# Layer A of a three-layer network: the projections' input kept by position classes modulo 4

## Chip, core and metric

One core of one Trainium2 chip runs the whole kernel. The metric is device time in microseconds (us), the median of several runs; lower is better.

## What is computed

A sequence of 512 positions with 1024 features goes through two layers, each a mixer and a mixture of experts with modulation from a condition vector, and then a third block with a state space and a pooling branch. All of it is float32. The change concerns the mixer of the first layer, "layer A":

```python
A_DILATED = ((128, 1), (512, 4), (2048, 16))   # window, dilation of the three groups

def dilated_group_attention(q, k, v, bias_table, window, dilation):
    """Query t attends to t - m*dilation, m = 0..window/dilation. Keys are gathered by stride:
    the sequence is split into `dilation` residue classes ..."""

def dilated_mixer(h, w_in, w_out, q_gain, k_gain, rel_bias):
    proj = (h @ w_in).reshape(b, s, A_N_GROUPS, 3, A_HEADS_PER_GROUP, HEAD_DIM)
    for g, (window, dil) in enumerate(A_DILATED):
        q = rmsnorm(proj[:, :, g, 0], q_gain) * ATTN_SCALE
        k = rmsnorm(proj[:, :, g, 1], k_gain)
        v = proj[:, :, g, 2]
        o, l = dilated_group_attention(q, k, v, tab, window, dil)
    ...
    wts = jax.nn.softmax(jnp.stack(lses, axis=0), axis=0)
    o = jnp.sum(wts[..., None] * outs, axis=0)
    return o.reshape(b, s, A_GROUP_WIDTH) @ w_out
```

Each group has 16 heads of 64 features. Group 0 attends to neighbouring positions; groups 1 and 2 attend within classes of positions that are equal modulo 4 (and 16).

## The kernel before

The normalized and modulated input of layer A lies transposed in SBUF, features on partitions, as `hT`: two float32r tiles `hThi` and `hTlo` of 128 x 8 x 512 whose sum is the float32 value. They are made in mix_a: tiles of x are normalized, transposed by TensorE and copied to `xT` (L2095), scaled and shifted to `hfull` (L2127), and split in two. Their 512 positions stand in natural order.

`dilated` goes through 24 units, for each of 8 pairs of heads the groups 0, 1, 2. A unit (`qkv_proj`) projects q, k and v of a pair of heads, 384 columns, for four tiles of 128 positions. Each tile adds up 8 blocks of 128 features, each in three terms (high x high, high x low, low x high): 96 pairs of a weight load and a matmul in a unit, all recorded at L153 (`split3`). The stationary operand of each is a slice of `hT`, the moving one the weights. Which positions make a tile is set in `qkv_part`: in group 0 tile t is the positions 128 t to 128 t + 127, in groups 1 and 2 it is every fourth position from t on:

```python
ts = slice(t, None, 4) if strided else slice(t * P, (t + 1) * P)
```

From a tile's sums in PSUM (`mm`, two buffers), ScalarE copies q and k to `raw` (L410), squares them to `sq` (L412) and copies v to `vhi` (L413); VectorE makes `vlo` (L414) and reduces the squares to `qss` (L415). Between the tiles the next unit's weights `wst` are split into `whi` and `wlo` (L315, L316). At the unit's end q and k are multiplied with the inverse norms (L425).

Attention runs as steps between the projections' matmuls. `qk_rows` transposes q and k (L435); for group 0 they are split into `qTh`, `qTl`, `kTh`, `kTl` (L448 to L452). `attn_near` computes group 0's scores (L536), the softmax pieces (L461, L462) and, in `attn_values`, the transposes of the probabilities (L474) and the products with v (L153, `av`) into `UN` (L551). `attn_far` does the same for groups 1 and 2 and writes its result in natural order to `UR`, at a step of four floats (L607). `merge` joins both. Besides, 20 blocks of the modulation of later stages are summed up on VectorE from `w_ada` (`ast`, `adacc`, L240 to L248).

TensorE's order is set by hand: `weave` mixes the projection's steps and the attention's steps by costs written in the source (490 for three pairs). The orders of the other engines and of SP's queue, which issues nearly all transfers, are set by the scheduler of the tile framework; each engine works in order. Layer B uses the same `qkv_proj` with natural tiles.

Of the kernel before, what the change touches and what calls it, by code (L numbers as in the profile page):

```python
# [9 lines left out]
F32 = mybir.dt.float32  # L10
# [10 lines left out]
S = 512  # L21
# [79 lines left out]
class Held:  # L101
    """Takes an engine's calls and keeps them for later."""
# [9 lines left out]
class Kernel:  # L112
# [47 lines left out]
    def rsqrt_exp(self, pool, out, v, n, tag, after):  # L160
        """exp(-ln(v) / 2), then a Newton step."""
        nc = self.nc
        t = self.t(pool, [P, n], F32, tag + "_t", 2)
        self.need_ln(after)
        with self.tc.issue_after(self.ln_table.ins):
            nc.scalar.activation(out, v, AF.Ln)
        nc.scalar.activation(out, out, AF.Exp, scale=-0.5)
        nc.vector.tensor_mul(t, out, out)
        nc.vector.scalar_tensor_tensor(t, t, -0.5, v, op0=ALU.mult, op1=ALU.mult)
        nc.vector.scalar_tensor_tensor(out, t, 1.5, out, op0=ALU.add, op1=ALU.mult)  # L170

# [11 lines left out]
    def first_columns(self, pool):  # L183
        """What the first modulation needs."""
# [47 lines left out]
    def ada_steps(self, pool, l, cb, st_tag="ast", n_st=2, later=False, n_acc=2, n_pe=0):  # L232
        """The last n_pe rows of blocks are TensorE's, the others are summed up on VectorE first."""
# [40 lines left out]
    def row(self, pool, col, tag, bufs=1):  # L274
        """A vector held one value per partition, as a row on every partition."""
# [11 lines left out]
    def tile_norm(self, pool, x):  # L287
        """1 / rms of every row of a tile."""
# [34 lines left out]
    def w_unit(self, w, base, ncols, qkv):  # L323
        """[k, 3 x 128 columns] of a projection: a pair of heads' q, k and v. The splits are left to do, piece by piece."""
# [11 lines left out]
    def w_rows(self, w, k0, nk, base, ncols, n, width=None, todo=None):  # L336
        """[k0 .. k0+nk, n columns] of a matrix, in one piece."""
# [9 lines left out]
    def weave(self, bg, fg):  # L347
        """bg yields costs (or what it has to wait for); fg holds (lane, steps, delay), and steps yield cost and delay.
        A lane's steps run one after the other."""
# [39 lines left out]
    def qkv_part(self, p, w, hT, strided, t, k):  # L389
        ts = slice(t, None, 4) if strided else slice(t * P, (t + 1) * P)  # L390
# [4 lines left out]
    def qkv_proj(self, pool, w, hT, strided, u, g, nv, todo, begun=None, n_raw=2):  # L395
        """begun: sums over the first features, where they have been started."""
# [3 lines left out]
        vlo = self.t(pool, [P, NT, P], F32R, f"vlo{g}", nv)  # L400
        raw = self.t(pool, [P, NT, 2, P], F32, "raw", n_raw)
        ss = self.t(pool, [P, 4 * NT], F32, "qss", n_raw)
        u.update(v=(vhi, vlo), raw=raw, ss=ss)
        for t in range(NT):
            p = ps[t] if ps else self.mm()
            for k in range(k0, KC):
                self.qkv_part(p, w, hT, strided, t, k)
# [3 lines left out]
            sq = self.t(pool, [P, 256], F32, "sq", 2)  # L411
# [4 lines left out]
            if t < NT - 1:  # L416
                for x in todo[t:t + 1] if t < 2 else todo[t:]:
                    self.split_weights(*x)
                yield 490
        v = self.t(pool, [P, 4 * NT], F32, "qv", 2)  # L420
# [7 lines left out]
    def qk_rows(self, pool, u, l, g, split):  # L428
        """q and k with heads' features on partitions."""
        nc = self.nc  # L430
        out = []
        for j, nm in enumerate(("qT", "kT")):
# [11 lines left out]
            else:  # L444
                hi = self.t(pool, [P, S], F32R, f"{nm}h{g}", 1)
                lo = self.t(pool, [P, S], F32R, f"{nm}l{g}", 1)
                if j == 0:
                    nc.scalar.activation(hi, p, AF.Copy, scale=gain)  # L448
                    nc.vector.scalar_tensor_tensor(lo, p, gain, hi.bitcast(F32), op0=ALU.mult, op1=ALU.subtract)
                else:  # L450
                    nc.scalar.activation(hi, p, AF.Copy)
                    nc.vector.tensor_sub(lo, p, hi.bitcast(F32))  # L452
# [5 lines left out]
    def softmax_piece(self, p, bias, out, z, d, n):  # L458
        """out = exp(p + bias - max), z = -max, d = the sum."""
# [4 lines left out]
    def transpose_split(self, pool, blocks, n, tag, q=P):  # L464
        """Transposes of q x 128 blocks of a float32 tile, in two parts."""
# [32 lines left out]
    def bias_rep(self, head):  # L498
        """The row of a head once per partition, so that rows shifted by one each can be read."""
# [15 lines left out]
    def attn_near(self, pool, u, hp, st):  # L515
        """Group 0 over its pair of heads: each block of 128 queries against its own and the block before."""
# [4 lines left out]
        yield from self.qk_rows(pool, u, 0, 0, True)  # L521
# [32 lines left out]
    def attn_values(self, pool, f, blocks, hs, terms, out):  # L554
        """Transposes of the probabilities' blocks, then their products with v; out(h, [64, S])."""
# [21 lines left out]
    def attn_far(self, pool, u1, u2, hp, st, out):  # L577
        """Groups 1 and 2 over their pairs of heads, by classes of positions mod 4; then the merge."""
# [34 lines left out]
    def merge(self, pool, UN, UR, st, out):  # L613
        """One softmax over both kinds of keys from their maxima and sums."""
# [62 lines left out]
    def dilated(self, keep, pool, hT, oT, first, begun, extra):  # L677
# [5 lines left out]
        def bg():  # L683
            nxt = first
            for i, (hp, g) in enumerate(units):
# [13 lines left out]
                if i >= back:  # L699
                    yield lambda p=hist[i - back][1], g=g: p.get("near" if g == 0 else "far")  # L700
                yield from self.qkv_proj(pool, cur[0], hT, g != 0, us[g], g, 2 if g == 1 else 1, nxt[1] if i + 1 < len(units) else [],
                                         None if i else begun)
# [33 lines left out]
    def out_start(self, keep, oT, w, done, scored):  # L736
        """All but the last heads' part of the first columns; done(k): those heads are through, scored(): all scores are."""
# [35 lines left out]
    def out_final(self, pool, x, mT, w, g):  # L773
        """x plus the last projection, its RMS norm, and out."""
# [56 lines left out]
    def route_in(self, h, hT, ks, rw, out):  # L831
        """Some columns' part in a tile's logits."""
# [9 lines left out]
    def route_tiles(self, pool):  # L842
        """What the routes are collected in."""
# [7 lines left out]
    def route_tile(self, pool, lg, R, t):  # L851
        """A tile's experts: its group, and the two best in it."""
# [5 lines left out]
        def first_max(v, m, o):  # L858
            """Largest of four, and a one-hot of the first place where it stands."""
# [20 lines left out]
    def route_rank(self, R, t):  # L880
        """Each token's rank with its experts, from one (zero: not its own)."""
# [6 lines left out]
    def route_counts(self, pool, R):  # L888
        """The experts' counts, and whether one is above the places."""
# [11 lines left out]
    def route_gates(self, pool, lg, R):  # L901
        """The gates, in three parts."""
# [26 lines left out]
    def token_list(self, pool, rk, idx, q=P):  # L929
        """By place, of q, the token whose rank it is (out of range where there is none)."""  # L930
# [27 lines left out]
    CAP = 96    # places of an expert; tokens beyond them go through overflow()  # L958

    def expert_loads(self, l):  # L960
        """Loads, six pieces an expert: two each of its gate, up and down."""
# [57 lines left out]
    def expert_hidden_T(self, pool, hid, w):  # L1019
        """Transposed: in two parts where the weights are, or as it is."""  # L1020
# [19 lines left out]
    def expert_out(self, pool, hT, d, idx, gate, R):  # L1040
        """Products with the down weights, times the gate and the modulation, added to x in DRAM."""
# [12 lines left out]
    def overflow(self, pm, R, hd, l):  # L1054
        """Tokens beyond an expert's places, 128 at a time, for any counts: run only where there are some."""
# [83 lines left out]
    def moe_route(self, x, l, rows, steps):  # L1139
        """steps makes x, a tile at a time."""  # L1140
# [54 lines left out]
    def moe(self, R, after):  # L1195
        """after() is called among the experts, for what the next layer can have early."""
# [77 lines left out]
    def normed_T(self, pool, xd, rows, hT):  # L1274
        """Tile by tile: the RMS norm (times a row, plus a row), transposed, in two parts."""
# [22 lines left out]
    def forget_rows(self, pool, hT):  # L1298
        """Minus the running sums of log sigmoid(f), per head: [16, S] in DRAM."""
# [906 lines left out]
```

## Time and profile before

| | |
|---|---|
| median of 3 runs | 1909.9 us (1907.71 to 1918.23) |
| span of the profiled execution | 1907.5 us, 2.4 us less than the median of the runs |
| TensorE busy | 92% of the span |
| VectorE, ScalarE, GpSimd busy | 67%, 48%, 6% |
| layer A's attention | from about 50 to 740 us |

The profiled execution has a time of its own only as that span, from its first to its last instruction. Engines are named PE (TensorE matmuls), PEld (TensorE's weight loads, which overlap the matmuls), DVE (VectorE), ACT (ScalarE), POOL (GpSimd) and SP (the queue that issues transfers). A matmul's recorded duration overlaps its neighbours'; what a pair of load and matmul costs is read from the step between two starts. A row of the waits names who waited for whom, the sum, how often and the longest. The granted clock is TensorE's, as a share of 2.4 GHz.

### The profile page before, as it was taken

How to read it: one execution, taken by the hardware profiler on the slowest of the kernel's cores; microseconds unless marked ns; L12 is line 12 of the kernel's file. 1: busy time of each engine (PE TensorE's matmuls, PEld its weight loads, DVE VectorE, ACT ScalarE, POOL GpSimd, SP SyncE). 2: the span in 40 equal slices, each digit the busy share in tenths (PEclk: the TensorE clock that was granted, in tenths of full speed). 3: DMA queues.
4: the chain of work that ended last, by engine and by line, in shares of the span. 5: the costliest groups of instructions: out<-in, count | busy, mean ns of one | idle time of the engine just before them, and what ended most of it. 6: DMA issues, size and time to landing. Idle time of an engine off the chain costs nothing. (4 is left out here: it accounts for less than half of the span.)

```text
span 1907.5 us, 30333 instructions
## 1 busy us (share of the span) xinstructions
PE 1753.2 (92%) x11022; PEld 1567.3 (82%) x11023; DVE 1280.8 (67%) x3181; ACT 920.1 (48%) x1978; POOL 119.5 (6%) x95
## 2 busy tenths in 40 slices
PE   5989999999999999699978999999599968999998
PEld 3989999999999998577757888979487748788886
DVE  6747657665765555788755758765687755998674
ACT  4535444453544454365634555554365544444443
POOL 1000000000000000122310000000123210000000
PEclk9999999999999999799989999989699988999999
DMA  8785535444453213699964321216499964333332
GB/s 282 224 263 151 158 108 155 144 142 128 142 160 106 84 56 117 205 300 311 304 182 115 110 55 56 78 34 211 134 321 316 304 179 120 94 103 95 100 112 87
DMA packets 283390, 302.45 MB, mean 159 GB/s; under 512 B 30751, under 2 KB 232075, under 8 KB 283228
## 3 DMA queue, kind: packets, MB, share of 16 engines
q1 hardware_dynamic: 275676, 283.49, 47.7%
q0 software_dynamic: 7552, 16.89, 4.0%
q8 instruction: 91, 1.49, 0.3%
q14 instruction: 71, 0.58, 0.1%
HBM read 283.42 MB, written 34.71 MB: 167 GB/s over the span
## 5 line engine op out<-in xcount | busy, mean ns | idle before, releaser
L153 PE MATMUL mm<-whi,hThi 128*128 128x384 f32 (+2 forms) x1128 | 438.7, 389 | 12.3 <-DVE vlo L414 9.1
L153 PE MATMUL mm<-whi,hTlo 128*128 128x384 f32 (+2 forms) x1128 | 413.7, 367 | 0.7
L153 PE MATMUL mm<-wlo,hThi 128*128 128x384 f32 (+2 forms) x1128 | 412.7, 366 | 0.0
L153 PEld LDWEIGHTS mm<-whi,hThi 128*128 128x128 f32 x1128 | 284.5, 252 | 20.8 <-DVE vlo L414 9.4
L153 PEld LDWEIGHTS mm<-whi,hTlo 128*128 128x128 f32 x1128 | 286.5, 254 | 5.9 <-DVE hTlo L728 3.0
L153 PEld LDWEIGHTS mm<-wlo,hThi 128*128 128x128 f32 x1128 | 287.6, 255 | 1.9 <-issue 0.6
L316 DVE TENSOR_TENSOR wlo<-wst,whi 128x768 fp32r<-128x768 f32 (+2 forms) x200 | 200.5, 1011 | 73.0 <-ACT whi L315 71.3
L315 ACT ACTIVATE whi<-wst 128x768 fp32r<-128x768 f32 (+2 forms) x200 | 176.3, 891 | 98.4 <-PE mm L153 64.4
L316 DVE TENSOR_TENSOR ehl<-est,ehl 128x1024 fp32r<-128x1024 f32 x144 | 175.7, 1222 | 51.4 <-ACT ehl L315 50.8
L315 ACT ACTIVATE ehl<-est 128x1024 fp32r<-128x1024 f32 x144 | 152.0, 1057 | 98.4 <-PE sc L153 31.6
L153 PE MATMUL mm<-ehl,xTh 128*96 128x256 f32 x960 | 178.4, 287 | 0.0
L248 DVE SCALAR_TENSOR_TENSOR adacc<-ast,csil,adacc 128x512 f32<-128x512 f32 x168 | 126.0, 750 | 54.6 <-DMA ast<-in_w_ada_dram 52.8
L153 PE MATMUL mm<-ehl,xTl 128*96 128x256 f32 x480 | 135.9, 283 | 0.0
L153 PEld LDWEIGHTS mm<-ehl,xTh 128*96 128x96 f32 x960 | 134.7, 165 | 0.0
L415 DVE TENSOR_REDUCE qss<-sq 128x4 f32<-128x256 f32 x128 | 53.0, 414 | 102.0 <-ACT sq L412 101.7
L410 ACT ACTIVATE raw<-mm 128x256 f32<-128x256 f32 x126 | 48.1, 382 | 145.3 <-PE mm L153 145.0
L153 PE MATMUL mm<-hThi,whi 128*128 128x512 f32 (+1 forms) x288 | 108.1, 375 | 0.7 <-ACT sza L1875 0.6
L153 PE MATMUL mm<-hTlo,whi 128*128 128x512 f32 (+1 forms) x288 | 106.7, 371 | 0.5 <-DVE hTlo L310 0.3
L153 PE MATMUL mm<-hThi,wlo 128*128 128x512 f32 (+1 forms) x288 | 106.5, 370 | 0.0
L153 PEld LDWEIGHTS mm<-ehl,xTl 128*96 128x96 f32 x480 | 79.0, 165 | 0.0
L1214 POOL MEMSET xg<- 96x1024 f32 x6 | 5.5, 951 | 1127.3 <-PE sc L153 1127.3
L954 POOL DMA_INDIRECT xd<-y,tidx x32 | 66.9, 2091 | 123.0 <-DVE hTl L1036 95.3
(486 smaller groups left out, 3543.5 us busy)
## 6 DMA issues: line engine op xcount, KB each, us to landing
ast<-in_w_ada_dram SPq DMA_DIRECT2D x192, 256.0 KB, 3.0
wst<-in_a_w_in_dram SPq DMA_DIRECT2D x192, 192.0 KB, 3.6
est<-in_w_gate_dram SPq DMA_DIRECT2D x64, 512.0 KB, 10.6
est<-in_w_up_dram SPq DMA_DIRECT2D x60, 512.0 KB, 11.3
wst<-in_w_in_dram SPq DMA_DIRECT2D x32, 512.0 KB, 4.0
est<-in_w_down_dram SPq DMA_DIRECT2D x30, 512.0 KB, 9.8
esp<-in_w_down_dram SPq DMA_DIRECT2D x30, 512.0 KB, 11.2
wst<-in_b_w_in_dram SPq DMA_DIRECT2D x64, 192.0 KB, 3.7
```

The costliest lines, as they stand in the source:

```text
L153: self.nc.tensor.matmul(out, lhsT=l, rhs=r, start=n_first and i == 0, stop=n_last and i == nt - 1)
L248: last = nc.vector.scalar_tensor_tensor(acc, st, self.csil[:, k:k + 1], acc, op0=ALU.mult, op1=ALU.add)
L315: nc.scalar.activation(hi, st, AF.Copy)
L316: nc.vector.tensor_sub(lo, st, hi.bitcast(F32))
L410: nc.scalar.activation(raw[:, t].rearrange("p a b -> p (a b)"), p[:, :256], AF.Copy)
L415: nc.vector.tensor_reduce(ss[:, 4 * t:4 * t + 4], sq.rearrange("p (g d) -> p g d", d=HD), axis=AX.X, op=ALU.add)
L954: self.nc.gpsimd.indirect_dma_start(out=dst, out_offset=bass.IndirectOffsetOnAxis(ap=idx, axis=0), in_=src, in_offset=None, bounds_check=S ...
L1214: nc.gpsimd.memset(xg, 0.0)
```

## The change

The transposed input of layer A is kept by classes of positions modulo 4: first all positions with remainder 0, then 1, 2 and 3. Every tile of every group is then 128 neighbouring columns of `hT`. Group 0's results are put back in natural order: q and k as they are split after their transposes, written at a step of four floats, v through a tile in DRAM, written in natural order by one transfer and read back by another, for each of its two halves. These four transfers of a pair of heads are issued on SP. One scratch tile, `sq`, goes from two buffers to one, and group 0's values get two more tiles, `vch` and `vcl`. All other lines of the diff take out comments and docstrings.

```diff
-    def qkv_part(self, p, w, hT, strided, t, k):
-        ts = slice(t, None, 4) if strided else slice(t * P, (t + 1) * P)
+    def qkv_part(self, p, w, hT, t, k):
+        ts = slice(t * P, (t + 1) * P)
...
-    def qkv_proj(self, pool, w, hT, strided, u, g, nv, todo, begun=None, n_raw=2):
+    def qkv_proj(self, pool, w, hT, u, g, nv, todo, begun=None, n_raw=2, regroup=False):
...
+        vout = vhi, vlo
+        if regroup:
+            vhi = self.t(pool, [P, NT, P], F32R, f"vch{g}", 1)
+            vlo = self.t(pool, [P, NT, P], F32R, f"vcl{g}", 1)
...
-        u.update(v=(vhi, vlo), raw=raw, ss=ss)
+        u.update(v=vout, raw=raw, ss=ss)
...
-            sq = self.t(pool, [P, 256], F32, "sq", 2)
+            sq = self.t(pool, [P, 256], F32, "sq", 1)
...
+        if regroup:
+            for nm, src, dst in zip("hl", (vhi, vlo), vout):
+                vd = self.t(self.dp, [S, P], F32, "vd" + nm, 2)
+                nc.sync.dma_start(vd.rearrange("(n r) d -> n r d", r=4), src.bitcast(F32))
+                nc.sync.dma_start(dst.bitcast(F32), vd.rearrange("(b p) d -> p b d", p=P))
...
-    def qk_rows(self, pool, u, l, g, split):
+    def qk_rows(self, pool, u, l, g, split, regroup=False):
+        ro = (lambda x: x.rearrange("p (n r) -> p r n", r=4)) if regroup else (lambda x: x)
+        ri = (lambda x: x.rearrange("p (r n) -> p r n", r=4)) if regroup else (lambda x: x)
...
-                    nc.scalar.activation(hi, p, AF.Copy, scale=gain)
-                    nc.vector.scalar_tensor_tensor(lo, p, gain, hi.bitcast(F32), op0=ALU.mult, op1=ALU.subtract)
+                    nc.scalar.activation(ro(hi), ri(p), AF.Copy, scale=gain)
+                    nc.vector.scalar_tensor_tensor(ro(lo), ri(p), gain, ro(hi.bitcast(F32)), op0=ALU.mult, op1=ALU.subtract)
                 else:
-                    nc.scalar.activation(hi, p, AF.Copy)
-                    nc.vector.tensor_sub(lo, p, hi.bitcast(F32))
+                    nc.scalar.activation(ro(hi), ri(p), AF.Copy)
+                    nc.vector.tensor_sub(ro(lo), ri(p), ro(hi.bitcast(F32)))
...
-        yield from self.qk_rows(pool, u, 0, 0, True)
+        yield from self.qk_rows(pool, u, 0, 0, True, True)
...
-                yield from self.qkv_proj(pool, cur[0], hT, g != 0, us[g], g, 2 if g == 1 else 1, nxt[1] if i + 1 < len(units) else [],
-                                         None if i else begun)
+                yield from self.qkv_proj(pool, cur[0], hT, us[g], g, 2 if g == 1 else 1, nxt[1] if i + 1 < len(units) else [],
+                                         None if i else begun, regroup=g == 0)
...
-            proj = lambda hp, wu, todo: self.qkv_proj(pq, wu[0], hT, False, hist[hp], 0, DL["nvb"], todo, n_raw=DL["nrb"])
+            proj = lambda hp, wu, todo: self.qkv_proj(pq, wu[0], hT, hist[hp], 0, DL["nvb"], todo, n_raw=DL["nrb"])
...
-                        nc.scalar.activation(xT[:, 4 * i:4 * i + 4, t * P:(t + 1) * P], p.rearrange("p (a b) -> p a b", b=P), AF.Copy)
+                        xc = xT[:, 4 * i:4 * i + 4].rearrange("p k (r n) -> p k r n", r=4)
+                        nc.scalar.activation(xc[:, :, :, t * 32:(t + 1) * 32], p.rearrange("p (k n r) -> p k r n", k=4, r=4), AF.Copy)
```

## Rows read from the trace of the kernel before

**Rows 1.** the page's busy time of TensorE: share of the span, instructions

```profile
PE 1753.2 (92%) x11022; PEld 1567.3 (82%) x11023; DVE 1280.8 (67%) x3181; ACT 920.1 (48%) x1978; POOL 119.5 (6%) x95
```

**Rows 2.** windows: each engine's busy us (x instructions), granted clock, DMA share, GB/s

```profile
60.00:120.00 60.00, 57.82 (x312) 56.73 (x312) 34.02 (x79) 26.92 (x70) 0.00 (x0) 1.00 0.86 258
120.00:131.00 11.00, 5.50 (x20) 5.50 (x21) 6.55 (x14) 1.15 (x5) 0.00 (x0) 0.69 0.83 256
131.00:700.00 569.00, 567.48 (x3681) 554.83 (x3680) 357.50 (x921) 278.53 (x729) 0.00 (x0) 1.00 0.44 132
1062.00:1300.00 238.00, 231.74 (x1600) 201.43 (x1598) 160.58 (x551) 129.55 (x326) 0.00 (x0) 0.96 0.21 63
```

**Rows 3.** weight loads in order of time, group 1: start, duration, engine, line

```profile
60.27 0.33 PEld L153 LDWEIGHTS mm<-whi,hTlo 128*128 128x128 f32 x1
...
70.79 0.33 PEld L153 LDWEIGHTS mm<-whi,hTlo 128*128 128x128 f32 x1
```

**Rows 4.** the same view, group 0's second unit

```profile
113.49 0.19 PEld L153 LDWEIGHTS mm<-wlo,hThi 128*128 128x128 f32 x1
...
117.31 0.19 PEld L153 LDWEIGHTS mm<-whi,hTlo 128*128 128x128 f32 x1
```

**Rows 5.** windows, columns as in rows 2: one period of three units

```profile
459.90:542.90 83.00, 83.00 (x538) 81.25 (x537) 54.24 (x138) 40.56 (x107) 0.00 (x0) 1.00 0.47 140
```

**Rows 6.** weight loads at the stop in group 0's second unit

```profile
125.50 0.29 PEld L153 LDWEIGHTS mm<-whi,hThi 128*128 128x128 f32 x1 [8.00 <-DVE vlo L414]
125.66 0.34 PEld L153 LDWEIGHTS mm<-wlo,hThi 128*128 128x128 f32 x1
...
129.51 0.33 PEld L153 LDWEIGHTS mm<-wlo,hThi 128*128 128x128 f32 x1
```

**Rows 7.** VectorE in order of time at that stop

```profile
123.62 0.75 DVE L248 SCALAR_TENSOR_TENSOR adacc<-ast,csil,adacc 128x512 f32<-128x512 f32 x1 [3.90 <-DMA ast<-in_w_ada_dram]
```

**Rows 8.** windows, columns as in rows 2: DMA share early and later

```profile
60.00:70.00 10.00, 10.00 (x43) 10.00 (x44) 7.52 (x20) 4.43 (x13) 0.00 (x0) 1.00 0.97 284
160.00:170.00 10.00, 10.00 (x75) 9.35 (x75) 6.58 (x18) 4.65 (x14) 0.00 (x0) 1.00 0.34 107
```

**Rows 9.** tiles: duration min/median/max ns, first and last start, forms

```profile
L607 ACT ACTIVATE UR<-av x16: 1067/1088/1112, 159.7 to 733.4; 64x512 f32<-64x512 f32 x16
L551 ACT ACTIVATE UN<-av x16: 588/591/594, 100.4 to 692.0; 64x512 f32<-64x512 f32 x16
L452 DVE TENSOR_TENSOR kTl<-tp,kTh x8: 691/692/692, 74.4 to 657.6; 128x512 fp32r<-128x512 f32 x8
```

**Rows 10.** in order of time: fourth pair of heads, keys, first scores

```profile
325.74 0.69 DVE L452 TENSOR_TENSOR kTl<-tp,kTh 128x512 fp32r<-128x512 f32 x1 [1.07 <-ACT kTh L451]
...
331.84 0.19 PEld L536 LDWEIGHTS sc<-kTh,qTh 64*128 64x128 f32 x2 [0.18 <-issue]
```

**Rows 11.** DMA issues: how many, KB each, median us from issue to landing

```profile
ud<-u SPq DMA_DIRECT2D x4, 256.0 KB, 4.1
yP<-yqd SPq DMA_DIRECT2D x4, 256.0 KB, 3.7
```

**Rows 12.** fourth pair of heads, group 0: last values made, their first product

```profile
315.56 0.29 DVE L414 TENSOR_TENSOR vlo<-mm,vhi 128x128 fp32r<-128x128 f32 x1
...
348.81 0.15 PEld L153 LDWEIGHTS av<-pTh,vhi 128*64 128x64 f32 x1
```

**Rows 13.** SP's waits, 150 to 700 us: us in total, times, longest

```profile
SPq L240 <- DVE adacc L246: 105.9, 15, 11.3
```

**Rows 14.** tile xT: its copies, and what reads them first

```profile
L2095 ACT ACTIVATE xT<-tp x8: 580/597/597, 19.2 to 28.8; 128x512 f32<-128x512 f32 x8
L2127 ACT ACTIVATE hfull<-xT,mod,scol x4: 798/799/813, 33.2 to 35.3; 128x512 f32<-128x512 f32 x4
```

**Rows 15.** waits, 50 to 100 us: us in total, times, longest

```profile
ACT sq L412 <- DVE qss L415: 1.7, 1, 1.7
```

More of the change, by code (lines that the diff above doesn't have):

```diff
@@ L406, in qkv_proj @@
             for k in range(k0, KC):
-                self.qkv_part(p, w, hT, strided, t, k)
+                self.qkv_part(p, w, hT, t, k)
                 if k < KC - 1:
```

## The prediction

> **What bounds the kernel now.** I read the page's busy times first: TensorE is busy for 1753.2 us of a 1907.5 us span [rows 1]. A mean over stages with different limits says little, so the table of windows comes next. Over layer A's attention the reader should look at one pair of numbers: between 131 and 700 us TensorE is busy for 567.48 of 569 us at the full granted clock (1.00, which is 2.4 GHz), with VectorE at 357.50 us (63%), ScalarE at 278.53 us (49%) and the DMA engines at 0.44 [rows 2]. TensorE runs back to back there, so what its instructions cost is what this stage costs. Only the start differs: from 60 to 131 us the DMA engines are at 0.86 and 0.83, and TensorE stands still once.
>
> The third view is TensorE's weight loads in order of time. In qkv_part the input's 128 positions are the stationary operand, loaded anew for each matmul of 384 columns. In a unit of group 1 (positions `t, t+4, ...`) a load takes 0.33 us and the next starts 0.2338 us later: from 60.27 to 70.79 us there are 45 steps, 10.52 / 45 [rows 3]. In a unit of group 0 (128 neighbouring positions) of the same tiles hThi and hTlo, with the same matmul, a load takes 0.19 us and the step is 0.1736 us: from 113.49 to 117.31 us, 22 steps, 3.82 / 22 [rows 4]. The only thing in the code that differs between these stretches is the step between positions. So groups 1 and 2 are bound by the load of the stationary operand, and group 0 is not.
>
> The Trainium skill, page "TensorE: Matmul & The Clock Gate", section "LDWEIGHTS (loading the stationary operand)", gives a load's time from its number of columns alone, and would have both loads alike; the rows differ by 0.14 us in duration, so the measurement decides against it here. Its page "SBUF — State Buffer", section "Door 1: The DMA port swizzle", says that SBUF is read in lines of 16 bytes and that a read which moves to a new line each time pays; four floats are such a line, and the rows agree with that.
>
> **The change, part by part.**
>
> *Contiguous loads.* Two groups of 8 pairs of heads are 16 units, each of 4 tiles x 8 feature blocks x 3 terms = 96 pairs of load and matmul: 1536 pairs. Each should fall from 0.2338 to 0.1736 us: 1536 x 0.0602 = 92.5 us, all on the path that sets the end, since TensorE has no gaps for it to fall into. Group 0's units keep their 0.1736 us. TensorE's order is written by hand from costs in the source, none of which changes, so the same instructions follow in the same order.
>
> *What is late next.* A period of three units (459.9 to 542.9 us) has 83.00 us of TensorE, 54.24 us of VectorE and 40.56 us of ScalarE [rows 5]. TensorE loses 2 x 96 x 0.0602 = 11.6 us of it, which leaves 71.4 us; VectorE would go to 76%. It stays under TensorE, but the slack of every hand-over shrinks. Two rows bound what TensorE then idles: this stage's own 1.5 us in 569 (0.3%, about 1.5 us of the shorter stage), and layer B, where the same projection runs with contiguous loads among attention and TensorE is busy 231.74 of 238 us [rows 2], so 2.6% idle, or about 13 us of the stage that is left (569 less 81). I take 4 us, nearer to this stage's own row, because the instructions are its own.
>
> *The crowded start.* At 117.5 us TensorE stops for 8.00 us on vlo [rows 6], because VectorE, which works in order, has stood 3.90 us for a modulation weight on its way in [rows 7]; after it 12 steps take 0.321 us each at the lower clock (the window's mean granted clock is 0.69 [rows 2]), which adds about 2 us. DMA share is 0.97 in the ten microseconds from 60 and 0.34 from 160 [rows 8]. The two strided units before that stop save 11.6 us, but data that arrive no sooner make the stop longer by as much as TensorE came early. From the one side nothing is lost and the stop of 10 us even goes, from the other all 11.6 us are given back. I take half, 5.8 us.
>
> *Queries and keys of group 0 put back in order.* Per pair of heads two ScalarE and two VectorE operations write 512 elements at a step of four floats. ScalarE's nearest rows are UR, written with that very step, at 1.09 us, and UN, the same size written densely, at 0.59 us [rows 9]; so +0.50 us each, 8 us over 16 on an engine that is half idle. No VectorE operation of before writes so; kTl takes 0.69 us dense [rows 9], and I bound the extra by zero and one more 0.69 us, at most 11 us in 16, and take ScalarE's +0.50. On the path they count only as latency: kTl starts at 325.74 us and the scores that need it at 331.84 us [rows 10], so some 5.4 us of cover, of which about 27 pairs x 0.06 = 1.6 us go with faster projections and some 2 us with the four slower steps. What is left, 1.8 us, hides it; with VectorE behind by more than that, it costs at most 1 to 2 us a pair of heads. I put it at zero, with the 4 us above as its reserve.
>
> *Values of group 0 through DRAM.* Per pair of heads SP gets four more transfers of 256 KB, a write and a read back for each half. The nearest rows are such a round trip in the last block: 4.1 us to land written, 3.7 us read back [rows 11]. Both halves in line are 15.6 us. The values are ready 0.29 us after 315.56 and their first product starts at 348.81 us [rows 12]: 33 us of cover, less some 6 us for the 100 faster pairs between. So TensorE never waits for them. What can wait is what stands behind them on SP: a read that waits for its write holds up the modulation's and projections' weights for some 4 us, twice a period. SP already stands for up to 11.3 us at a time for a free buffer [rows 13] without TensorE stopping after 131 us. The four transfers are 1 MB among the 11.6 MB that 140 GB/s moves in 83 us. Cost: between zero and 2 x 4 us a period if VectorE has no slack, so up to 64 us; I take zero, as the row with the longer SP wait does no harm.
>
> *Small ones.* The eight xT copies (0.60 us each, the last at 28.8 us) now read and write in steps; +0.5 us each delays the last to about 33 us, just where hfull starts at 33.2 us [rows 14], so 0 to 1 us. With one sq buffer, ScalarE's square waits for VectorE's reduction of the tile before, 4.2 us earlier at least (24 pairs x 0.1736); with two it waited once, for 1.7 us [rows 15]. Layer B shares this line: 0 to 2 us there. Both at zero.
>
> **Sum.** -92.5 + 5.8 + 4.0 = -82.7 us. The profiled span of 1907.5 lies 2.4 us under the median of the runs, 1909.9, and I count the same distance again: 1909.9 - 82.7 = 1827 us.
>
> **The rivals.**
> *Better than the sum*: the stop at 117 us goes altogether and nothing idles: 1909.9 - 92.5 - 10 = 1807. For it: group 0's stretches already run without gaps. Against it: the DMA shares of the start. Chance 0.07.
> *A new wait takes the gain*: the chain of the stop (a late weight holds VectorE, vlo holds TensorE, then the lower clock), now fed by SP's round trips, recurs each period at 8 + 2 us. Four of eight give 1827 + 40 = 1867, all eight 1907. For it: VectorE's queue is in order and does wait for these weights. Against it: the DMA engines stand at 0.44 after 131 us. Chance 0.10.
> *It doesn't do what it says*: the load's time hangs on something other than the step (by the columns rule above, it would). The stage stays, and the additions cost 0 to 8 us: 1910 to 1918. Against it: same tiles, same matmul, 0.2338 against 0.1736. Chance 0.03.
> *Slower*: the values come back late. The cover is 27 us, the round trips 15.6; if SP holds the read back behind a blocked load, every microsecond over 27 is TensorE's, and it decides at 27 + 11.6 = 39 us, where the period is as long as before. At 45 us, 8 x 6 = 48 us longer: 1958. It needs about 29 us of queueing; the waits above reach 11.3. Chance 0.03.
> The forecast itself has 0.77.
>
> **How the numbers follow.** The forecast's own range is 1818 (nothing given back) to 1848 (11.6 and 13 us given back, 8 us of the small ones). The range reaches to the better case at 1807 and into the new wait at 1860. A measurement of this kernel tells about 0.5% (9.5 us) from no change. Faster by more: 0.77 + 0.07 + 0.08 of the new wait = 0.92. Within: 0.02 of it and 0.02 of the third = 0.04. Slower: 0.04.
>
> **What would show it.** In the profile after, the loads of all qkv units step by 0.174 us and none lasts 0.33 at the full clock; layer A's attention is about 80 us shorter; TensorE's busy share there stays above 97%; the strided writes take about 1.1 us; the values land long before their product. The prediction is wrong if TensorE's waits for vlo, scores or values add up to more than some 20 us in that stage, or if the DMA share of the start reaches 1 and the first period keeps its length.

## The result, and the profile after

The changed kernel takes 1849.28 us (median of 4 runs, 1845.19 to 1858.89) against 1911.37 us of the kernel before (4 runs, 1907.71 to 1918.23): a ratio of 0.9667, 95% interval 0.964 to 0.9694. The time lies inside the range, 22 us above the 1827 us that were forecast, and 1 us above what the forecast itself allowed (1818 to 1848). The profiled execution spans 1846.8 us, 60.7 us less than before.

First the page of the kernel after, busy time by engine: beside [rows 1] TensorE's busy time fell by 87.5 us, while VectorE's and ScalarE's grew by 1.8 and 6.4 us.

```profile
span 1846.8 us, 30370 instructions
PE 1665.7 (90%) x11022; PEld 1469.2 (80%) x11023; DVE 1282.6 (69%) x3181; ACT 926.5 (50%) x1978; POOL 121.0 (7%) x95
```

Then its weight loads in order of time, in a unit of group 1, where [rows 3] had 0.33 us (start, duration, engine, line):

```profile
59.90 0.19 PEld L153 LDWEIGHTS mm<-whi,hThi 128*128 128x128 f32 x1
...
66.48 0.19 PEld L153 LDWEIGHTS mm<-whi,hTlo 128*128 128x128 f32 x1
```

From the first to the last are 38 steps in 6.58 us, 0.173 us each: the step of [rows 4]. Over the whole steady stretch the loads of `mm` have a mean of 188 ns. The mechanism does what the prediction said.

The windows of the kernel after (stretch, length, then busy us and instructions of PE, PEld, DVE, ACT, POOL, granted clock, DMA share, GB/s) show what came of it; [rows 2] has the same view of before:

```profile
60.00:130.00 70.00, 57.39 (x355) 54.99 (x354) 41.81 (x93) 29.96 (x78) 0.00 (x0) 0.90 0.91 280
130.00:160.00 30.00, 27.29 (x204) 25.48 (x204) 22.70 (x57) 16.25 (x41) 0.00 (x0) 1.00 0.81 247
160.00:650.00 490.00, 473.58 (x3540) 451.07 (x3540) 347.43 (x889) 276.14 (x705) 0.00 (x0) 1.00 0.52 154
475.90:549.70 73.80, 71.62 (x538) 68.43 (x537) 54.34 (x139) 41.40 (x106) 0.00 (x0) 1.00 0.57 170
549.70:620.10 70.40, 70.36 (x538) 68.30 (x537) 44.76 (x123) 41.28 (x106) 0.00 (x0) 1.00 0.36 112
```

TensorE no longer runs back to back: it is idle for 16.4 of 490 us in the steady part. The last two lines are two neighbouring periods of three units. In the first VectorE still sums up modulation blocks; in the second there are none left, VectorE is busy 9.6 us less, and TensorE idles 0.04 us instead of 2.2.

The best ruler is the tile `oT`: its product of `UN` and `UR` closes each pair of heads, eight times (duration, first and last start). Of the kernel after, the sixth and the seventh:

```profile
L672 DVE TENSOR_TENSOR oT<-UN,UR x1: 683/683/683, 549.7 to 549.7; 128x512 f32<-128x512 f32 x1
L672 DVE TENSOR_TENSOR oT<-UN,UR x1: 685/685/685, 620.1 to 620.1; 128x512 f32<-128x512 f32 x1
```

All eight, read in the same way, in us (the third line is the last experiment below):

| | first pair ends | five periods, to the sixth | sixth to seventh | to the eighth |
|---|---|---|---|---|
| before | 184.1 | 415.7 | 81.7 | 57.4 (at 738.9) |
| after | 178.0 | 371.7 | 70.4 | 50.1 (at 670.2) |
| after, without most of the modulation sums | 160.0 | 352.5 | 70.5 | 50.1 (at 633.1) |

Layer A's attention ends 68.7 us earlier. The period without modulation gained 11.3 us, nearly the 11.6 us that 192 pairs were to give; each of the five periods with modulation gained only 8.8; and the start gained 6.1.

This ruler is good to about a microsecond. It stands on VectorE, and in the kernel before, the seventh product comes a little earlier in TensorE's order: its sixth-to-seventh stretch holds 526 TensorE instructions, against 538 in the kernel after.

```profile
599.80:681.50 81.70, 81.70 (x526) 80.02 (x524) 44.52 (x122) 40.53 (x106) 0.00 (x0) 1.00 0.27 80
```

Read at the same load of TensorE's order in both kernels, the start gains 7.3 us, the five periods 44.5, the sixth period 12.1 and the rest 4.7.

Later stages do the same work in both kernels. From `oT` to the first read of layer B's mixer there are 259.9 us before and 260.5 after, in the mixer of layer B 299.0 and 307.3, in the rest 609.7 and 608.8. So 68.7 - 0.6 - 8.3 + 0.9 = 60.7 us.

The waits of TensorE in the kernel after, 160 to 650 us (who waited for whom: us in total, times, longest), name the small stalls:

```profile
PE tp L668 <- DVE pTl L488: 6.2, 6, 1.3
PE tp L447 <- DVE raw L435: 2.7, 5, 0.7
PE tp L486 <- DVE nat L644: 2.6, 5, 1.1
PE sc L605 <- DVE sR L473: 2.0, 2, 1.2
PE sc L548 <- DVE zN L473: 1.1, 3, 0.5
```

All are waits for VectorE, and together they are 14.6 of the 16.4 us; the longest is 1.3 us. At the start the stop of [rows 6] is still there, in another place. In order of time, VectorE and then TensorE (start, duration, then in brackets the idle time before and what ended it):

```profile
120.31 0.75 DVE L248 SCALAR_TENSOR_TENSOR adacc<-ast,csil,adacc 128x512 f32<-128x512 f32 x1 [6.17 <-DMA ast<-in_w_ada_dram]
...
124.16 1.12 PE L447 MATMUL tp<-cst,raw 128*128 128x128 f32 x4 [6.11 <-DVE raw L435]
```

VectorE stands 6.17 us for a modulation weight, and `raw`, which waits behind it in VectorE's order, stops TensorE for 6.11 us.

### The profile page after: what moved, and what is told of

Its sections match the earlier page's. It is cut to its first block, busy times and chain, and to the rows that moved or that the text cites. A ratio compares the mean times of both kernels' runs of the same rounds, so it can differ in the third digit from the quotient of the medians.

```text
span 1846.8 us, 30370 instructions
## 1 busy us (share of the span) xinstructions
PE 1665.7 (90%) x11022; PEld 1469.2 (80%) x11023; DVE 1282.6 (69%) x3181; ACT 926.5 (50%) x1978; POOL 121.0 (7%) x95
## 5 line engine op out<-in xcount | busy, mean ns | idle before, releaser
L153 PE MATMUL mm<-whi,hThi 128*128 128x384 f32 (+2 forms) x1128 | 403.3, 358 | 5.4 <-ACT hThi L739 2.0
L153 PE MATMUL mm<-whi,hTlo 128*128 128x384 f32 (+2 forms) x1128 | 384.3, 341 | 1.0 <-DVE hTlo L740 0.5
L153 PE MATMUL mm<-wlo,hThi 128*128 128x384 f32 (+2 forms) x1128 | 382.6, 339 | 0.0
L153 PEld LDWEIGHTS mm<-whi,hThi 128*128 128x128 f32 x1128 | 215.6, 191 | 13.9 <-ACT hThi L739 3.2
L153 PEld LDWEIGHTS mm<-whi,hTlo 128*128 128x128 f32 x1128 | 214.9, 191 | 6.2 <-DVE hTlo L740 3.3
L153 PEld LDWEIGHTS mm<-wlo,hThi 128*128 128x128 f32 x1128 | 216.0, 191 | 1.9 <-issue 0.6
```

The lines of the kernel that those rows point to most:

```text
L153: self.nc.tensor.matmul(out, lhsT=l, rhs=r, start=n_first and i == 0, stop=n_last and i == nt - 1)
```

## Experiments

The theories, with the letters of the text (in the first three expectations "Theory B" is C here, and "Theory A" leaves open which of A and B holds; A1 and A2 are A and B). A: attention's steps now come too early for VectorE, because their places are set in costs of the source while the pairs between them got cheaper; longer delays would give the idle time back. B: VectorE itself is too late, since modulation sums stand in its queue, whatever the order of the steps. C: the additions (strided writes, values through DRAM, one `sq`) cost what is missing. Totals move by some us in later stages whatever is done in layer A, so each run is read by the end of layer A's attention (after: 670.2 us).

**The loads alone.** The kernel before, with neighbouring columns for every unit and none of the additions:

```diff
-        ts = slice(t, None, 4) if strided else slice(t * P, (t + 1) * P)
+        ts = slice(t * P, (t + 1) * P)
```

> The kernel before with one line changed: every unit takes 128 neighbouring positions, so groups 1 and 2 are computed on the wrong positions; no value, query or key is put back, sq keeps two buffers, xT is copied densely. It is the gain of the loads with none of the additions. Theory A (TensorE's steps got shorter than VectorE can follow, whatever is added): the time is near the changed kernel's, 1840 to 1855, with some 12 to 16 us of TensorE idle between 160 and 650 us and periods of 74 us. Theory B (the additions, that is the round trip on SP, the strided writes, the single sq, cost the missing 20 to 30 us): 1815 to 1830, periods near 71.5 us.

1841.24 us (ratio 0.9613, 0.9573 to 0.9653); attention ends at 668.2 us, with periods of 73.4 to 74.0 us and TensorE idle for 14.7 us between 160 and 650 us, as its theory A had it. The loads alone lose 21.8 of their 92.5 us. C is nearly out: all additions together are worth 2.0 us in layer A.

**The loads strided again.** The kernel after with every fourth column for groups 1 and 2, all additions kept:

```diff
-        ts = slice(t * P, (t + 1) * P)
+        ts = slice(t, None, 4) if g else slice(t * P, (t + 1) * P)
...
```

> The changed kernel with strided loads put back in groups 1 and 2 (which then take wrong positions): all additions without the gain. Theory A: the additions hide behind a TensorE that is the bound, so within 5 us of the kernel before, 1908 to 1916, periods 83 us. Theory B: 1925 to 1940. If layer B's loss of 8 us comes from the single sq, 1916 to 1920 under either, lost after layer A's attention.

Attention ends at 740.6 us against 738.9 of before: the step between columns is the whole of the gain, and the additions cost 1.7 us when loads are slow. The total, 2088.85 us, can't be used: 776 us pass after the end of layer B's attention instead of 610, with TensorE busy for 9.63 of the 100 us from 1400. I take it that other tokens meet other experts and a path for tokens beyond an expert's places runs; that is an inference.

**Without the round trip of the values.**

```diff
         if regroup:
-            vhi = self.t(pool, [P, NT, P], F32R, f"vch{g}", 1)
-            vlo = self.t(pool, [P, NT, P], F32R, f"vcl{g}", 1)
...
-                vd = self.t(self.dp, [S, P], F32, "vd" + nm, 2)
-                nc.sync.dma_start(vd.rearrange("(n r) d -> n r d", r=4), src.bitcast(F32))
-                nc.sync.dma_start(dst.bitcast(F32), vd.rearrange("(b p) d -> p b d", p=P))
+                pass
```

> The changed kernel without the values' way through DRAM: group 0's products take the values as they stand, in class order, so its results are wrong. Theory A: 1842 to 1850, the trip is hidden. Theory B with the trip as the cost: 1825 to 1835, most of it in the first 150 us, where the DMA engines are full.

1846.52 us (0.9639, 0.96 to 0.9678), attention ends at 668.4 us. The 32 transfers of 256 KB cost 1.8 us.

**Two `sq` buffers in layer B.** Layer B's mixer is the other place where time came back, and the change's only edit there is this buffer.

```diff
-            sq = self.t(pool, [P, 256], F32, "sq", 1)
+            sq = self.t(pool, [P, 256], F32, "sq", 2 if n_raw == 3 else 1)
```

> The changed kernel with two sq buffers in layer B alone (in layer A there is no room for the second). If the single sq costs layer B its 8 us: about 1841. If that loss is the clock, which fell to one half for ten microseconds there, and not the buffer: 1846 to 1850, with the lower clock somewhere in layer B again or not.

1855.89 us (0.9695, 0.9652 to 0.9737); layer B's mixer takes 306.4 us. The buffer is not the reason. The total lies above both expectations, as the stage between layer A's attention and layer B's mixer took 266.3 us, 5.8 longer than in the kernel after.

**Longer delays.** Theory A's own remedy, all eight delays of layer A's steps times 1.35:

```diff
+for _k in ('u', 'uf', 'q', 's', 'p', 't', 'v', 'm'):
+    DL[_k] *= 1.35
```

> The changed kernel with layer A's delays in the hand-written order of TensorE (u, uf, q, s, p, t, v, m) multiplied by 1.35, about the ratio of a strided to a contiguous step averaged over three units, so that attention's steps come as many microseconds after their inputs as they did before. Theory A1 (the idle of the steady part is the shrunken distance between VectorE's results and TensorE's steps): TensorE's 16 us of idle between 160 and 650 us fall below 6, and the time to 1834 to 1842. Theory A2 (VectorE itself is too full at 73%): the idle stays, and the longer chain of the last heads adds to it: 1849 to 1860.

1932.42 us (1.0081, 1.0052 to 1.011), attention ends at 758.0 us, the five periods take 87.5 to 93.5 us, and TensorE idles for 63 us between 160 and 650. I had not counted that in the source a unit's projections start only when attention of an earlier pair is done; that the longer chain holds them up is read from the source and not tested. The run says nothing against A or for it.

**Late bias rows.** For the start: the eight rows of biases of each later pair are issued behind the last weight load of the unit before (the lines that note this load are left out here).

```diff
...
-                    for h in range(2):
-                        self.bias_rep(2 * hp + h)
+                    with self.tc.issue_after(self.unit_ld[3 * hp - 1].ins) if hp > 1 else ExitStack():
+                        for h in range(2):
+                            self.bias_rep(2 * hp + h)
```

> The changed kernel with the sixteen writes of the bias rows to DRAM (wrep, 576 KB each) spread over the pairs of heads instead of nearly all in the first 130 us; each stands on SP behind the last weight load of the unit before. If the start is bound by the bandwidth of the DMA engines: their share between 60 and 130 us falls to about 0.65, the idle of TensorE between 50 and 160 us from 15 us to under 6, and the time to 1839 to 1843. If it is the two buffers of the modulation's weights and their latency: the idle stays, 1847 to 1851.

1849.57 us (0.9654, 0.9622 to 0.9686). The DMA share from 60 to 130 us falls from 0.91 to 0.75, the first pair ends at 172.4 instead of 178.0 us, attention at 663.8. From 50 to 130 us VectorE stands 9.5 us for modulation weights instead of 17.8. TensorE's idle time between 50 and 160 us falls from 15.7 to 11.5 us, between the two expectations (under 6, or as before). The crowded start is real, and its transfers are part of it. The total shows nothing of it, because later stages were longer by as much (from layer A's attention to layer B's mixer 263.7, layer B's mixer 307.1, the rest 612.9 us).

**Both of these**, the edits of the last two kernels in one.

> Both edits, longer delays and late rows, on the changed kernel. If the start and the steady part are two separate losses, the gains add up: 1824 to 1833. If one is only the other's shadow: no better than the better of the two alone.

1926.92 us (1.0064, 1.004 to 1.0088): the long delays decide.

**The kernel after once more**, with no edit, to see what recurs.

> The changed kernel again, unchanged, beside the others: 1845 to 1853. In its trace layer B, from the first load of its input to the last of its attention results, took 307.3 us against 299.0 before. If that is the clock of that execution, this one may give another number; if it is a matter of the program, 306 to 308 again.

1848.33 us (0.9649, 0.9618 to 0.968), attention ends at 670.3 us, layer B's mixer takes 305.3, just under the 306 to 308 expected if the program is the cause. Both findings recur, with 2 us between the two executions.

**Slightly longer delays**, times 1.12, on the run with late rows:

```diff
+for _k in ('u', 'uf', 'q', 's', 'p', 't', 'v', 'm'):
+    DL[_k] *= 1.12
```

> The kernel after with the row writes of the biases spread as in the run with late rows, and all eight hand-set delays of layer A's attention steps (u, uf, q, s, p, t, v, m) longer by 12%, a third of the lengthening tried before. Theory A (steps now come sooner than the results they need, because TensorE's real time per step shrank while the delays did not): TensorE's idle time between 160 and 650 us falls from 16 us to some 8 us, the waits of the transposes of the last merge step for VectorE fall below 3 us, and layer A's attention ends near 656 us instead of 663.8. Rival (the idle time is VectorE's and ScalarE's own latency between tiles, whatever the order): attention ends within 2 us of 663.8. A third possibility, that the longer chain of delays already blocks the projections: attention ends later than 668 us. Total 1838 to 1850 us, since later stages have moved by up to 8 us between kernels.

1894.68 us (0.9916, 0.9887 to 0.9946), attention ends at 717.2 us. The five periods are 81.6 to 83.7 us, and TensorE idles for 40.8 us between 160 and 650: it waits for other steps of VectorE (14.0 us for `zN` alone). The third possibility of the expectation.

**Only the merge later**, on the run with late rows:

```diff
+DL['m'] = 7.4
```

> The kernel after with late rows, and one delay alone longer: the one between the merge's sums and its transposes, from 5.95 to 7.4. Nothing blocks on this step, so the chain of delays can't hold the projections. Theory A: the waits of the merge's transposes for VectorE (6.5 us in the attention stage with late rows) go to under 1 us, attention ends 4 to 6 us earlier, near 658 to 660 us. Rival: TensorE's wait only changes its place (another step waits for the same late VectorE), attention ends at 663 to 664 us.

1863.3 us (0.9747, 0.9721 to 0.9774), attention ends at 679.6 us, 15.8 us later. TensorE's waits of this run, 160 to 650 us:

```profile
PE tp L489 <- DVE UN L673: 10.2, 7, 1.8
PE mm L155 <- DVE vlo L422: 5.7, 7, 1.3
PE tp L450 <- DVE raw L438: 3.1, 5, 0.9
PE tp L489 <- DVE nat L647: 2.4, 5, 0.9
```

The wait of the merge's transposes for `pTl` is gone, as A had it, and two larger ones for VectorE stand in its place. The idle time grew from 15.7 to 25.3 us. This is the rival, and worse. A falls as a remedy: moving steps only moves the wait.

**Modulation two units later**, on the kernel after:

```diff
+DL['xa'] = 4
```

> The kernel after with the modulation blocks that VectorE sums up beside layer A's attention begun two units later (from the fourth unit on instead of the second), so that their weights do not come in while the first three units' weights and biases do. Theory of the crowded start: VectorE does not wait for modulation weights before 130 us, the DMA share of 60 to 130 us falls from 0.91 to about 0.8, and layer A's attention ends 4 to 7 us earlier than in the kernel after, near 663 to 666 us. Rival (the bias rows and unit weights alone make the start slow): the end stays within 2 us of 670.

1853.07 us (0.9688, 0.9661 to 0.9714). The first pair ends at 171.8 us, 6.2 earlier, but attention at 672.6, 2.4 later. The start was not freed as the theory had it: before 130 us VectorE still stands 21.5 us for modulation weights (17.8 in the kernel after), and the DMA share is 0.89. The later end the expectation missed as well: the modulation now reaches into the period from the sixth pair to the seventh. Its window:

```profile
546.30:620.90 74.60, 71.95 (x538) 68.56 (x537) 54.29 (x138) 41.37 (x106) 0.00 (x0) 1.00 0.52 157
```

In the kernel after this period took 70.40 us with 44.76 us of VectorE. So the extra 4.2 us travel with the modulation sums, which speaks for B.

**One block of modulation in eight**, on the kernel after; VectorE loses 7/8 of the sums beside layer A's attention, and SP and the DMA engines the transfers for them:

```diff
-        for k in range(KC):
+        for k in range(1 if later is True else KC):
```

> The kernel after, leaving out a part of the computation: the modulation blocks summed up beside layer A's attention take only the first of their eight blocks of features, so that VectorE loses some 88 us of its 347 us between 160 and 650 us, and 7 of 8 of the weight transfers of these blocks go. The modulation of all later stages is not the reference's (and so may be the routing of the tokens); only layer A's attention is read. Theory: TensorE's idle time in the steady part is VectorE's in-order queue being behind (its results and the PSUM buffers it frees come late because modulation sums and waits for their weights stand ahead of them). Then the 16.4 us of idle time between 160 and 650 us fall below 6 us, the start's waits for raw and vlo go below 3 us, and attention ends at 648 to 655 us instead of 670.2. Rival: the idle time is the latency from TensorE through ScalarE and VectorE and back in attention's own steps, whatever else VectorE does: idle stays at 12 us or more, attention ends at 660 to 668 us.

Attention ends at 633.1 us, 37.1 earlier and 15 earlier than the best that was expected. (The one total, 1805.01 us, lacks work.) Its windows, and then its longest waits of TensorE from 160 to 630 us:

```profile
60.00:130.00 70.00, 66.69 (x447) 64.51 (x446) 39.92 (x108) 38.79 (x106) 0.00 (x0) 0.98 0.90 275
160.00:630.00 470.00, 467.14 (x3548) 451.42 (x3547) 269.43 (x763) 271.03 (x694) 0.00 (x0) 1.00 0.32 93
```

```profile
PE sc L605 <- DVE sR L473: 0.7, 1, 0.7
PE mm L153 <- DVE hTlo L740: 0.6, 2, 0.3
PE mm L153 <- ACT hThi L739: 0.5, 1, 0.5
```

Six periods of 70.5 us with the same steps in the same places on TensorE: idle time falls from 16.4 in 490 to 2.9 in 470 us, and the delays were long enough all along. At the start the DMA share is as high as ever (0.90), yet TensorE is busy 66.69 of 70 us. So it is modulation's share of VectorE, not the share of the DMA engines as such, through which the start is slow. B holds. What this run doesn't tell apart is the sums themselves (88 us of VectorE between 160 and 650) from VectorE's waits for their weights (42 us there): it takes both away, and the transfers with them.

The trace of the kernel after tells a part of it. Ahead of each of the five waits for `raw` a sum stands among VectorE's steps, and VectorE waits for no weight there; one of them, VectorE and then TensorE:

```profile
519.89 0.75 DVE L248 SCALAR_TENSOR_TENSOR adacc<-ast,csil,adacc 128x512 f32<-128x512 f32 x1
...
521.25 1.22 DVE L435 TENSOR_TENSOR raw<-raw,qr 128x1024 f32<-128x1024 f32 x1
522.62 0.63 PE L447 MATMUL tp<-cst,raw 128*128 128x128 f32 x4 [0.48 <-DVE raw L435]
```

Ahead of each of the five waits for `nat` VectorE stands 0.7 to 1.4 us for a weight. So both occur. Directly ahead of the largest, `pTl`, stand steps of the merge and a weight split, and no sum; how the modulation makes it late is not shown.

No version that does all of the work beat the changed kernel by more than a measurement can tell.

## Why the prediction was right, and where its sum was off

- **Contiguous loads, 92.5 us.** Right in mechanism and size. 0.2338 to 0.173 us a pair; the period without modulation gives 11.3 of 11.6 us (12.1 at the same places of TensorE's order). The Trainium skill, page "TensorE: Matmul & The Clock Gate", section "LDWEIGHTS (loading the stationary operand)", gives a load's time from its columns; by that rule nothing would have changed, and the same 128 columns went from 0.33 to 0.19 us. The third rival, which doesn't do what it says, is out.
- **What is late next, 4 us.** This is the step that failed. In five periods 10 units were to give 57.8 us and gave 44.0, so 13.8 us are lost, and 0.3 more in the sixth period. The prediction saw VectorE go to 76% of the period (it is 54.34 of 73.80 us, 74%) and took TensorE's own idle share from a stage where VectorE had been at 63%. The upper end, layer B's 2.6%, gave 13 us and was the better row: there, too, VectorE works at 67% beside contiguous projections [rows 2]. The measured share is 3.3%.
- **The crowded start, 5.8 us.** Right in mechanism, mis-sized: four units outside the five and the sixth period were to give 23.1 us, the stretch behind the seventh pair gave 7.3 and the start 6.1, so 9.7 are lost, near the upper bound of 11.6. At the same places of TensorE's order all of it is the start's: of its 306 strided pairs 18.4 us were to come, and 7.3 came. The stop did not go; it moved from 117.5 to 118 us and from `vlo` to `raw`. That VectorE standing for a modulation weight causes the stop was right: the rows above show it in the kernel after, and the first pair ends 18 us earlier in the last experiment, where most of these weights are gone.
- **Strided writes, nothing on the path.** Right. ScalarE's take 1.20 and 1.11 us, near the 1.09 us of `UR` in [rows 9], and VectorE's `kTl`, which also reads `kTh` at this step, 0.40 us more than in [rows 9] where 0.50 was taken. All additions of layer A cost about 2 us where zero was put and 8 were kept in reserve. The kernel after, first pair, in order of time:

```profile
71.96 1.20 ACT L460 ACTIVATE qTh<-tp,gqk 128x512 fp32r<-128x512 f32 x1 [1.46 <-PE tp L447]
73.18 1.17 DVE L461 SCALAR_TENSOR_TENSOR qTl<-tp,gqk,qTh 128x512 fp32r<-128x512 f32 x1 [1.05 <-ACT qTh L460]
74.26 1.11 ACT L463 ACTIVATE kTh<-tp 128x512 fp32r<-128x512 f32 x1 [1.11 <-PE tp L447]
75.40 1.09 DVE L464 TENSOR_TENSOR kTl<-tp,kTh 128x512 fp32r<-128x512 f32 x1 [1.05 <-ACT kTh L463]
```

- **Values through DRAM, nothing of 0 to 64 us.** Right, 1.8 us. In the fourth pair the write is issued at 294.74 us and the read back at 298.55, and the first product starts at 323.30: 28.6 us of cover, some 27 forecast. So the slower rival had no ground.
- **A new wait takes the gain (1867 to 1907).** A weaker form of it came: VectorE, behind with modulation, does hold TensorE up in each period. But not by one stop of 10 us. A period with modulation is 3.4 us longer than the one without (73.80 and 70.40 us); of these TensorE's idle time, in waits of at most 1.3 us, is 2.1, and its busy time for the same 538 instructions is 1.3 longer.
- **Small ones, nothing.** `xT`'s copies still take 0.60 us. The single `sq` does not lengthen layer B's mixer.
- **Not in the sum at all: layer B's mixer, 8.3 us longer.** The engines do the same work there (VectorE 199.59 and 200.12 us), TensorE is idle for 17.1 and 17.4 us, and one thing differs, the granted clock. The kernel before, the run with the loads alone, and the kernel after:

```profile
998.80:1297.80 299.00, 281.91 (x1874) 245.90 (x1875) 199.59 (x642) 156.19 (x392) 0.00 (x0) 0.95 0.26 76
```

```profile
929.00:1228.50 299.50, 282.09 (x1873) 245.91 (x1874) 199.57 (x642) 156.02 (x391) 0.00 (x0) 0.95 0.26 76
```

```profile
930.70:1238.00 307.30, 289.87 (x1873) 251.73 (x1874) 200.12 (x642) 156.37 (x391) 0.00 (x0) 0.92 0.25 74
992.00:1002.00 10.00, 9.31 (x56) 7.49 (x54) 6.42 (x17) 3.94 (x13) 0.00 (x0) 1.00 0.42 123
1002.00:1012.00 10.00, 10.00 (x35) 7.59 (x35) 6.61 (x26) 4.61 (x13) 0.00 (x0) 0.50 0.17 53
1012.00:1022.00 10.00, 10.00 (x87) 9.23 (x86) 5.57 (x10) 6.47 (x13) 0.00 (x0) 0.99 0.00 0
```

For 10 us TensorE goes at 1.2 GHz (0.50) and executes 35 instructions, after ten microseconds in which it was busy for 9.31; the kernel before, at the same place of the stage, ran on at 1.00:

```profile
1060.00:1070.00 10.00, 9.80 (x58) 8.09 (x58) 6.49 (x20) 4.32 (x15) 0.00 (x0) 1.00 0.33 100
1070.00:1080.00 10.00, 9.99 (x73) 8.41 (x72) 8.19 (x29) 7.16 (x19) 0.00 (x0) 1.00 0.16 52
```

A second place adds to it: from 1050 to 1060 us the kernel after is granted 0.50 for the whole 10 us, and the kernel before for 3.5 us at the same place (0.51 from 1116.3 to 1119.8). Eleven executions of kernels with all or some of the additions took 302.9 to 307.3 us there; the twelfth, with one block of modulation in eight, took 300.9, with PE and VectorE busy as in the kernel before. So the additions as such don't force it; it differs between executions whose work in this stage is the same.

Of the signs named beforehand, the loads, the strided writes and the values came as said. TensorE's busy share from 160 to 650 us is 96.6%, where above 97% was named, and attention is 68.7 us shorter, where about 80 was. The forecast's own upper end was added up wrongly: 1909.9 - 92.5 + 11.6 + 13 + 8 is 1850, not 1848, and the result lies just inside it.

Of the 22 us between forecast and result, 9.8 + 0.3 are VectorE's hand-over, 3.9 the start, and 8.0 the later stages, layer B's clock above all: 92.5 - 13.8 - 0.3 - 9.7 - 8.0 = 60.7.

**What stays open.** Why the clock falls at other places of layer B's mixer in the kernels with the additions. That the single `sq` does it is excluded. Two executions of the same kernel differ, too (307.3 and 305.3 us). And how the loss divides between the two halves of the modulation's load on VectorE, sums and waits for weights.

## What to carry to other kernels

A stationary operand read at a step can cost more than the same columns side by side: compare the step between two starts of the same matmul before you trust a price by columns. When the engine at the bound gets faster by a seventh, do not take its idle share from the stage as it was; look for work on the next engine that comes and goes (here the modulation sums) and compare a period with it and one without. And if the waits are all for one engine's in-order queue, moving the waiting steps moves the wait; taking work out of that queue removes it.

## What was not expected of the hardware

A load of 128 float32r columns at a step of four floats takes 0.33 us, side by side 0.19 us, and sets the pace of a pair at 0.234 against 0.173 us. VectorE's operation for `kTl`, 128 x 512, which now writes its result and reads `kTh` at a step of four floats, takes 1.09 us where the dense one took 0.69 us [rows 9]. And TensorE fell to half its clock for 10 us in a stretch where it had been busy for 9.31 of the 10 us before, while the kernel before, busy for 9.80 of 10 us at the same place, stayed at the full clock.
